# Half of the modulation vector moves from VectorE to TensorE, in the opening of a trunk kernel

## The chip, the cores and the metric

One NeuronCore of a Trainium2 chip runs the whole program. The time is device microseconds of one execution. PE is TensorE, DVE is VectorE, ACT is ScalarE, POOL is GpSimd, SP is SyncE, which here only issues DMAs.

## The reference, cut to what matters

One layer of a hybrid trunk: 2048 tokens, 1024 features, 8 heads of an RWKV7 mixer and 8 heads of chunked band attention. Its normalised input is scaled and shifted by a modulation vector that is made from a conditioning vector `c`:

```python
c_act = jax.nn.silu(c)
mod = c_act @ w_ada[l] + b_ada[l]                    # (1024) @ (1024, 3072)
shift, scale, gate = jnp.split(mod, 3, axis=-1)
h = rms_norm(x, norm_g[l]) * (1.0 + scale[:, None, :]) + shift[:, None, :]
proj = h @ w_in[l]
...
x = x + gate[:, None, :] * (y @ w_out[l])
```

So no token's projection can start before the parts of `shift` and `scale` that belong to its features are there. `w_ada` for shift and scale is 8 MB in f32.

## The kernel before

Features lie on partitions, in KT = 8 blocks of P = 128 (index k); tokens are taken 512 at a time. Matmuls of the projection keep f32 accuracy by splitting both operands into a high and a low part (`hh`, `hl` for h; `whi`, `wlo` for the weights) and making three 512-wide matmuls, lines L130 to L132, helper `gemm_k`.

`phase_a` projects and attends; `phase_r`, the recurrence, follows. Phase A's *opening* is what the change touches. It loads the first 512 tokens of x (eight tiles `hx`), sums their squares (`ssx` on DVE, `ps_ss` by four one-column matmuls on PE), takes the power -0.5 on POOL (`r`), spreads it over partitions (`rbx` on ACT, `ps_rx` by four transposes on PE, `rsb` on ACT), and multiplies all eight x tiles by it on POOL (`hx`, L309). Then a loop over k makes, for each block of features, two columns of the modulation vector `modv`, and with them h and its share of four projections that add up in the four PSUM tiles `ps_first`:

- `mod_part` loads two tiles `wada` of 128 x 1024 (half a megabyte each; seven buffers), scale first, then shift. In each, partition p holds the 1024 weights of output feature p, and DVE multiplies it by `sil`, which is silu(c) on every partition, and adds along the row (L146, a custom operation and a short read of the sum). L148 adds the bias.
- `g1` = (1 + scale) times the norm's gain (L405, DVE).
- `build_k` makes `hh` (ACT, L370), takes it from the full product (DVE, L371), and makes `hl` (ACT, L373).
- `split` loads the weights of this k (`raw`), and makes `whi` on ACT (L122) and `wlo` on POOL (L111).
- 12 wide matmuls: four projections, three products each.

The wada loads are issued from SP's queue, held behind the last load of x. Four casts of a zero tile into `pth` and `ptl` (L422, L423) stand behind the opening in the code, but belong to no step of it. Within phase A a scheduler sets the order of instructions on each engine when the kernel is built, by its own estimate of the times; on the chip each engine takes its instructions strictly in that order. Behind the opening PE goes on with the projections and the attention of the same tokens.

The gate half of `mod` is made much later, in `gate()`: DVE accumulates weights whose *input* features lie on partitions, times a column of `silc` (silu(c) with features on partitions), and PE adds over the partitions in one-column matmuls, `ps_gate`.

Of the kernel before, what the change touches and what calls it, by code (L numbers as in the profile page):

```python
# [9 lines left out]
F32 = mybir.dt.float32  # L10
F32R = mybir.dt.float32r
BF16 = mybir.dt.bfloat16
AF = mybir.ActivationFunctionType
ALU = mybir.AluOpType
# [4 lines left out]
P = 128  # L19
# [3 lines left out]
S = 2048  # L23
D = 1024
KT = D // P
# [47 lines left out]
def body(tc, nc, x, xT, wi, wadaT, wadaG, wo, sc, cst, bx, w2, a2, cb, eyes, outT):  # L73
    ctx = ExitStack()
    with ctx:
        pool = lambda name, st=ctx, **k: st.enter_context(tc.tile_pool(name=name, **k))
        cp = pool("cp", bufs=1)
        dp = pool("dp", bufs=1, space=DRAM)
        wx = pool("wx", bufs=2)
        psp = pool("psp", bufs=2, space=PSUM)  # L80

        y_d = dp.tile([NP, P, S], F32, name="y_d")
        ar_d = dp.tile([NP, P, 2 * S], F32, name="ar_d")
        kb_d = dp.tile([NP, P, 2 * S], F32, name="kb_d")
        bv_d = dp.tile([NP, P, S], F32, name="bv_d")
        v_d = dp.tile([NP, P, S], F32, name="v_d")
        sg_d = dp.tile([NP, P, S], F32, name="sg_d")

        sct = cp.tile([P, NSC], F32, name="sct")
        nc.sync.dma_start(out=sct, in_=sc)  # L90
        cs = cp.tile([P, NCP], F32, name="cs")
        nc.sync.dma_start(out=cs, in_=cst[:, 0:NCP])
        col = lambda n, i: sct[:, SC[n][0] + i:SC[n][0] + i + 1]
        cols = lambda n: sct[:, SC[n][0]:SC[n][1]]
        C = lambda n: cs[:, CS[n][0]:CS[n][1]]
        ident = C("ident")
        dv = cp.tile([P, 52], F32, name="dv")
        _d = [0]

        def derived(w):  # L100
            o = _d[0]
            _d[0] += w
            return dv[:, o:o + w]

        nhalf = cp.tile([P, 16], F32, name="nhalf")
        nc.gpsimd.memset(nhalf, -0.5)
        one = cp.tile([P, 1], F32, name="one")
        nc.gpsimd.memset(one, 1.0)

        def sub(eng, out, full, hi):  # L110
            eng.tensor_tensor(out=out, in0=full, in1=hi.bitcast(F32), op=ALU.subtract)  # L111

        ld1 = [None]

        def split_half(src, q):
            return split(src[:, q * 512:(q + 1) * 512])

        def split(src):
            raw = wx.tile([P, 512], F32, name="raw", tag="raw", bufs=3)
            ld1[0] = nc.sync.dma_start(out=(raw if len(src.shape) == 2 else raw.rearrange("p (a b) -> p a b", b=src.shape[2])), in_=src)  # L120
            hi = wx.tile([P, 512], F32R, name="whi", tag="whi", bufs=3)
            nc.scalar.copy(out=hi, in_=raw)  # L122
            lo = wx.tile([P, 512], F32R, name="wlo", tag="wlo", bufs=3)
            sub(nc.gpsimd, lo, raw, hi)
            return hi, lo

        def gemm_k(ps, w, h, k, kw, first, last):
            (wh, wl), (hh, hl) = w, h
            f = slice(kw * P, kw * P + P)
            nc.tensor.matmul(ps, lhsT=wh[:, f], rhs=hh[:, k, :], start=first, stop=False)  # L130
            nc.tensor.matmul(ps, lhsT=wh[:, f], rhs=hl[:, k, :], start=False, stop=False)  # L131
            nc.tensor.matmul(ps, lhsT=wl[:, f], rhs=hh[:, k, :], start=False, stop=last)  # L132

        def gemm(ps, src, h):
            ws = [split_half(src, q) for q in range(2)]
            for k in range(KT):
                gemm_k(ps, ws[k // 4], h, k, k % 4, k == 0, k == KT - 1)

        modv = cp.tile([P, 24], F32, name="modv")
        wcall = cp.tile([P, NP, S // 64], F32, name="wcall")  # L140

        def mod_part(wp, sil, ms):
            for m in ms:
                w = wp.tile([P, D], F32, name="wada", bufs=7)
                nc.sync.dma_start(out=w, in_=wadaT[m])
                nc.vector.tensor_tensor_reduce(out=w, in0=w, in1=sil, scale=1.0, scalar=0.0, op0=ALU.mult, op1=ALU.add,  # L146
                                               accum_out=modv[:, m:m + 1])
                nc.vector.tensor_tensor(out=modv[:, m:m + 1], in0=modv[:, m:m + 1], in1=col("bada", m), op=ALU.add)  # L148

        g1 = derived(8)  # L150
        q = phase_a(tc, nc, locals())
        phase_r(tc, nc, locals(), q)

# [131 lines left out]
def phase_a(tc, nc, e):  # L285
    x, xT, wi, bx, cst, cb, wadaG, w2, a2 = (e[k] for k in ("x", "xT", "wi", "bx", "cst", "cb", "wadaG", "w2", "a2"))
    C, col, cols, ident, derived = (e[k] for k in ("C", "col", "cols", "ident", "derived"))
# [4 lines left out]
    with st:  # L292
# [9 lines left out]
        def pst(name):  # L302
            return ps_t.tile([P, 512], F32, name=name, tag="pt")
# [28 lines left out]
        def load_x0():  # L332
            acc = W("ssx")
            xts = []
            for k in range(KT):
                t = W("hx")
                ld = nc.sync.dma_start(out=t, in_=xT[k, :, 0:TA])
                xts.append(t)
                sq = acc if k == 0 else ap.tile([P, 512], F32, name="sqx", tag="xt", bufs=2)
                nc.scalar.activation(sq, t, AF.Square)  # L340
                if k:
                    nc.vector.tensor_tensor(out=acc, in0=acc, in1=sq, op=ALU.add)
            ps = pst("ps_ss")
            for i in range(4):
                nc.tensor.matmul(ps[:, i:i + 1], lhsT=acc[:, i * P:(i + 1) * P], rhs=one, start=True, stop=True)
            s4 = ap.tile([P, 4], F32, name="s4", bufs=2)
            return xts, rms(s4, ps[:, 0:4]), ld
# [43 lines left out]
        mp = pool("mp", mst, bufs=1, side="right")  # L391
        sil = mp.tile([P, D], F32, name="sil")
        nc.sync.dma_start(out=sil, in_=cb)
        xts, rb0, ld0 = load_x0()
        sth = mp.tile([P, D], F32, name="sth", tag="wada", bufs=7)
        nc.scalar.activation(sth, sil, AF.Tanh, scale=0.5)
# [2 lines left out]
        rsb = finish_x(rb0)  # L399
        h0 = h_tiles()  # L400
        first = [psp.tile([P, 512], F32, name=f"ps_first{i}", tag="pj") for i in range(2)] + [pst("ps_first2"), pst("ps_first3")]
        with tc.issue_after(ld0.ins):
            for k in range(KT):
                mod_part(mp, sil, (8 + k, k))
                nc.vector.scalar_tensor_tensor(out=g1[:, k:k + 1], in0=modv[:, 8 + k:9 + k], scalar=1.0, in1=col("ng", k),  # L405
                                               op0=ALU.add, op1=ALU.mult)
                build_k(0, k, rsb, h0, xts[k])
                w = split(wi[17:30:4, :, k * P:(k + 1) * P].rearrange("f p c -> p f c"))
                for j in range(4):
                    gemm_k(first[j], w, h0, k, j, k == 0, k == KT - 1)  # L410
# [311 lines left out]
            nc.sync.dma_start(out=sg_d[p, :, tsl], in_=gr)  # L722

        def gate():
            silc = derived(8)
            nc.scalar.activation(silc, cols("c"), AF.Tanh, scale=0.5)
            nc.vector.tensor_scalar(out=silc, in0=silc, scalar1=0.5, scalar2=0.5, op0=ALU.mult, op1=ALU.add)
            nc.vector.tensor_tensor(out=silc, in0=silc, in1=cols("c"), op=ALU.mult)
            for hf in range(2):
                acc = W("gacc")  # L730
                for k in range(KT):
                    w = wx.tile([P, 512], F32, name="raw", tag="raw", bufs=3)
                    nc.sync.dma_start(out=w, in_=wadaG[k, :, hf * 512:hf * 512 + 512])
                    if k == 0:
                        nc.vector.tensor_scalar(out=acc, in0=w, scalar1=silc[:, 0:1], scalar2=None, op0=ALU.mult)
                    else:
                        nc.vector.scalar_tensor_tensor(out=acc, in0=w, scalar=silc[:, k:k + 1], in1=acc, op0=ALU.mult, op1=ALU.add)
                    if k % 2 == 1:
                        yield
                ps = pst("ps_gate")  # L740
                for m in range(4):
                    nc.tensor.matmul(ps[:, m:m + 1], lhsT=acc[:, m * P:(m + 1) * P], rhs=one, start=True, stop=True)
                o = 16 + 4 * hf
                nc.vector.tensor_tensor(out=modv[:, o:o + 4], in0=ps[:, 0:4], in1=cols("bada")[:, o:o + 4], op=ALU.add)
                yield
# [371 lines left out]
def layout(a):  # L1117
# [12 lines left out]
    dist = 128 + np.arange(P)[:, None] - np.arange(256)[None, :]  # L1130
    idx = np.clip(dist, -63, 128) + 63
    return {
        "x": x.reshape(16, P, D), "xT": x.T.reshape(KT, P, S), "wi": wt(f["w_in"][0]), "wadaT": f["w_ada"][0].T.reshape(24, P, D)[:16], "wadaG": f["w_ada"][0][:, 2 * D:].reshape(KT, P, D),
        "wo": wt(f["w_out"][0]), "sc": np.concatenate([parts[n] for n in SC], axis=1), "cst": consts(),
        "cb": np.broadcast_to(f["c"][0], (P, D)), "bx": rb[:, idx].transpose(1, 0, 2), "w2": f["w2"][0], "a2": f["a2"][0],
        "eyes": np.repeat(np.eye(32, dtype=np.float32).reshape(16, 2, 32).transpose(1, 0, 2).reshape(2, 512), 64, axis=0),
# [19 lines left out]
```

## Time and profile before

| | |
|---|---|
| median of 3 executions | 1775.95 us (1772.7 to 1777.89) |
| the profiled execution | 1771.38 us, span 1769.6 us |
| last matmul of the opening ends | 64.53 us |
| PE busy in the span | 1553.7 us, 88% |
| DVE busy in the span | 1090.2 us, 62% |

The profile is that of one execution. The span is from its first to its last recorded instruction; starts are counted from its beginning. A row of the timeline gives the start, the busy time, engine, line, operation, the tiles written and read, shapes, how many instructions it sums up, and in brackets how long the engine stood idle before it and what released it. An f32 matmul leaves two records, an fp32r one leaves one. Matmuls overlap in the pipeline: what one costs in a dense run is the distance between starts.

### The profile page before, as it was taken

The page shows a single profiled execution, that of the slowest core. Times are in us where ns is not written, and L with a number is a line of the kernel's source. Part 1 is how long each engine was busy: PE and PEld are TensorE (multiplying, and loading weights), DVE is VectorE, ACT ScalarE, POOL GpSimd, SP SyncE. Part 2 cuts the span into 40 slices and gives each one's busy share as a digit, 9 for nine tenths or more (in the row PEclk, how much of TensorE's full clock was granted, in tenths as well). Part 3 has the DMA queues.
Part 4 walks back from the last instruction along what each step waited for, and adds up shares of the span by engine and source line. Part 5 has one row for each costly group of instructions (what it writes and reads, how often), then busy time and mean ns, then how long its engine had stood idle before and what let it go on. Part 6 is the DMA issues. An engine that isn't in the chain of part 4 may idle for free. (4 is left out here: it accounts for less than half of the span.)

```text
span 1769.6 us, 32130 instructions
## 1 busy us (share of the span) xinstructions
PE 1553.7 (88%) x11944; PEld 1270.9 (72%) x11944; DVE 1090.2 (62%) x2407; ACT 929.9 (53%) x2087; POOL 708.4 (40%) x571
## 2 busy tenths in 40 slices
PE   3899998899999899999979999978688889889795
PEld 2677876678777678888868878856576667767685
DVE  7647457475576846746566574576555576566732
ACT  3666556566555565656566666652234344444440
POOL 4455544555444455444536544505212121221221
PEclk9999999899999999999999999999788999899897
DMA  8463333332324523223142332255746665664532
GB/s 286 130 222 102 100 114 101 114 119 73 113 93 135 167 72 125 81 93 114 60 137 72 126 102 66 66 192 159 229 129 183 167 195 154 187 183 122 148 115 90
DMA packets 188957, 231.60 MB, mean 131 GB/s; under 512 B 62976, under 2 KB 101632, under 8 KB 188800
## 3 DMA queue, kind: packets, MB, share of 16 engines
q1 hardware_dynamic: 183552, 212.76, 39.6%
q0 software_dynamic: 5248, 16.78, 2.7%
q8 instruction: 94, 1.54, 0.4%
q14 instruction: 63, 0.52, 0.1%
HBM read 171.30 MB, written 58.20 MB: 130 GB/s over the span
## 5 line engine op out<-in xcount | busy, mean ns | idle before, releaser
L111 POOL TENSOR_TENSOR wlo<-raw,whi 128x512 fp32r<-128x512 f32 x272 | 369.9, 1364 | 424.4 <-ACT whi L122 374.9
L122 ACT CAST whi<-raw 128x512 fp32r<-128x512 f32 x272 | 167.6, 618 | 173.9 <-issue 53.5
L130 PE MATMUL ps_r<-hh,whi 128*128 128x512 f32 x544 | 219.5, 404 | 13.8 <-ACT carry L632 10.6
L132 PE MATMUL ps_r<-hh,wlo 128*128 128x512 f32 x544 | 218.1, 401 | 2.2 <-POOL wlo L111 2.2
L131 PE MATMUL ps_r<-hl,whi 128*128 128x512 f32 x544 | 218.1, 401 | 0.0
L130 PE MATMUL ps_qkvg<-hh,whi 128*128 128x512 f32 x480 | 196.0, 410 | 10.7 <-ACT carry L632 7.1
L131 PE MATMUL ps_qkvg<-hl,whi 128*128 128x512 f32 x480 | 194.4, 406 | 9.0 <-DVE hl L377 5.3
L132 PE MATMUL ps_qkvg<-hh,wlo 128*128 128x512 f32 x480 | 192.7, 402 | 0.4 <-POOL wlo L111 0.4
L111 DVE TENSOR_TENSOR ptl<-ps_pt,pth 128x384 fp32r<-128x384 f32 (+1 forms) x232 | 105.2, 473 | 43.5 <-ACT pth L598 42.9
L130 PEld LDWEIGHTS ps_r<-hh,whi 128*128 128x128 f32 x544 | 103.5, 190 | 34.8 <-ACT carry L632 11.4
L588 ACT ACTIVATE sp<-sp,mn 128x640 f32<-128x640 f32 (+4 forms) x128 | 97.9, 765 | 53.9 <-DVE mn L584 53.0
L132 PEld LDWEIGHTS ps_r<-hh,wlo 128*128 128x128 f32 x544 | 103.3, 190 | 24.8 <-POOL wlo L111 3.1
L131 PEld LDWEIGHTS ps_r<-hl,whi 128*128 128x128 f32 x544 | 103.5, 190 | 20.1
L130 PEld LDWEIGHTS ps_qkvg<-hh,whi 128*128 128x128 f32 x480 | 92.0, 192 | 32.8 <-ACT carry L632 8.5
L131 PEld LDWEIGHTS ps_qkvg<-hl,whi 128*128 128x128 f32 x480 | 91.9, 191 | 31.1 <-DVE hl L377 7.5
L598 ACT CAST pth<-ps_pt 128x384 fp32r<-128x384 f32 (+1 forms) x232 | 90.8, 416 | 42.8 <-PE ps_pt L595 39.9
L132 PEld LDWEIGHTS ps_qkvg<-hh,wlo 128*128 128x128 f32 x480 | 92.2, 192 | 21.0 <-POOL wlo L111 0.6
L595 PE MATMUL ps_pt<-cs,sp 128*128 128x128 f32 x560 | 94.5, 281 | 10.8 <-DVE ptl L111 4.3
L604 PE MATMUL ps_o<-ptl,vc 128*128 128x256 f32 x336 | 92.5, 301 | 9.5 <-DVE ptl L111 9.5
L603 PE MATMUL ps_o<-pth,vc 128*128 128x256 f32 x336 | 92.2, 295 | 8.2 <-ACT pth L598 5.9
L1019 POOL DMA_DIRECT2D out<-xres x40 | 22.3, 557 | 173.3 <-DVE xres L1018 131.6
L582 DVE CUSTOM_DVE_ANT_0 sp<-ps_sa,mab 128x384 f32<-128x384 f32 (+1 forms) x112 | 58.7, 524 | 43.4 <-PE ps_sa L558 26.8
(256 smaller groups left out, 3713.5 us busy)
## 6 DMA issues: line engine op xcount, KB each, us to landing
raw<-in_wi SPq DMA_DIRECT2D x264, 256.0 KB, 2.9
hx<-in_xT SPq DMA_DIRECT2D x32, 256.0 KB, 5.4
wada<-in_wadaT SPq DMA_DIRECT2D x16, 512.0 KB, 8.7
ar_d<-art SPq DMA_DIRECT2D x16, 512.0 KB, 3.7
kb_d<-kbt SPq DMA_DIRECT2D x16, 512.0 KB, 3.2
kb<-kb_d SPq DMA_DIRECT2D x8, 1024.0 KB, 5.9
ar<-ar_d SPq DMA_DIRECT2D x8, 1024.0 KB, 6.4
xres<-in_xT SPq DMA_DIRECT2D x32, 256.0 KB, 3.4
```

Of the source, the lines that this page charges most:

```text
L111: eng.tensor_tensor(out=out, in0=full, in1=hi.bitcast(F32), op=ALU.subtract)
L122: nc.scalar.copy(out=hi, in_=raw)
L130: nc.tensor.matmul(ps, lhsT=wh[:, f], rhs=hh[:, k, :], start=first, stop=False)
L131: nc.tensor.matmul(ps, lhsT=wh[:, f], rhs=hl[:, k, :], start=False, stop=False)
L132: nc.tensor.matmul(ps, lhsT=wl[:, f], rhs=hh[:, k, :], start=False, stop=last)
L582: nc.vector.tensor_tensor_reduce(out=sp[:, 0:na], in0=sa[:, 0:na], in1=m_ap, scale=1.0, scalar=3e38, op0=ALU.add, op1=ALU.min, accum_out=m ...
L588: nc.scalar.activation(sp[:, 0:n], sp[:, 0:n], AF.Exp, scale=-1.0, bias=mn[:, 1:2], accum_out=ls[:, 2 * v + hh_:2 * v + hh_ + 1])
L595: nc.tensor.transpose(pp[:, kk - lo, :], sp[:, kk * P:(kk + 1) * P], ident)
L598: nc.scalar.copy(out=ph, in_=pp)
L603: nc.tensor.matmul(po[:, hh_, :], lhsT=wv_, rhs=pth[:, m, :], start=(m == m0), stop=False)
L604: nc.tensor.matmul(po[:, hh_, :], lhsT=wv_, rhs=ptl[:, m, :], start=False, stop=(m == 5))
L1019: nc.gpsimd.dma_start(out=dst[m, :, tsl], in_=xt)
```

## The change

The host lays out the scale half of `w_ada` with the input features on partitions. `mod_part` then makes the scale column of block k on PE: eight f32 matmuls, each with a 128 x 128 piece of the weight tile as stationary operand and one column of `silc` as moving operand, add up in column k of one PSUM tile, `ps_mod`. The bias add reads that column (L152). The shift half is made as before. `silc` is made ahead of the opening rather than in `gate()`.

```diff
-        def mod_part(wp, sil, ms):
-            for m in ms:
-                w = wp.tile([P, D], F32, name="wada", bufs=7)
-                nc.sync.dma_start(out=w, in_=wadaT[m])
-                nc.vector.tensor_tensor_reduce(out=w, in0=w, in1=sil, scale=1.0, scalar=0.0, op0=ALU.mult, op1=ALU.add,
-                                               accum_out=modv[:, m:m + 1])
-                nc.vector.tensor_tensor(out=modv[:, m:m + 1], in0=modv[:, m:m + 1], in1=col("bada", m), op=ALU.add)
+        def mod_part(wp, sil, silc, ps, k):
+            w = wp.tile([P, D], F32, name="wada", bufs=7)
+            nc.sync.dma_start(out=w, in_=wadaT[8 + k])
+            for i in range(KT):
+                nc.tensor.matmul(ps[:, k:k + 1], lhsT=w[:, i * P:(i + 1) * P], rhs=silc[:, i:i + 1], start=(i == 0), stop=(i == KT - 1))
+            w = wp.tile([P, D], F32, name="wada", bufs=7)
+            nc.sync.dma_start(out=w, in_=wadaT[k])
+            nc.vector.tensor_tensor_reduce(out=w, in0=w, in1=sil, scale=1.0, scalar=0.0, op0=ALU.mult, op1=ALU.add,
+                                           accum_out=modv[:, k:k + 1])
+            nc.vector.tensor_tensor(out=modv[:, k:k + 1], in0=modv[:, k:k + 1], in1=col("bada", k), op=ALU.add)
+            nc.vector.tensor_tensor(out=modv[:, 8 + k:9 + k], in0=ps[:, k:k + 1], in1=col("bada", 8 + k), op=ALU.add)
...
+        silc = derived(8)
+        nc.scalar.activation(silc, cols("c"), AF.Tanh, scale=0.5)
+        nc.vector.tensor_scalar(out=silc, in0=silc, scalar1=0.5, scalar2=0.5, op0=ALU.mult, op1=ALU.add)
+        nc.vector.tensor_tensor(out=silc, in0=silc, in1=cols("c"), op=ALU.mult)
...
+        ps_mod = pst("ps_mod")
         with tc.issue_after(ld0.ins):
             for k in range(KT):
-                mod_part(mp, sil, (8 + k, k))
+                mod_part(mp, sil, silc, ps_mod, k)
...
         def gate():
-            silc = derived(8)
-            nc.scalar.activation(silc, cols("c"), AF.Tanh, scale=0.5)
-            nc.vector.tensor_scalar(out=silc, in0=silc, scalar1=0.5, scalar2=0.5, op0=ALU.mult, op1=ALU.add)
-            nc.vector.tensor_tensor(out=silc, in0=silc, in1=cols("c"), op=ALU.mult)
```

The scheduler sets a new order. On PE, at the start of the program, this stood before; the names are the PSUM tile written, then the moving and the stationary operand, and the brackets name the engines and DMA queues waited for:

```order
L345 MATMUL ps_ss<-one,ssx 128x1 x3
L319 MATMUL ps_rx<-cs,rbx 128x128 [waits DMAHW1_49,Activation_49]
L319 MATMUL ps_rx<-cs,rbx 128x128 x3
L130 MATMUL ps_first_163<-hh,whi 128x512 [waits Activation_49]
L130 MATMUL ps_first_164<-hh,whi 128x512
```

This stands there now:

```order
L323 MATMUL ps_rx<-cs,rbx 128x128 [waits DMAHW1_49,Activation_49]
L323 MATMUL ps_rx<-cs,rbx 128x128 x3
L146 MATMUL ps_mod<-dv,wada 128x1 [waits DMAHW3_49]
L146 MATMUL ps_mod<-dv,wada 128x1 x7
L146 MATMUL ps_mod<-dv,wada 128x1 [waits DMAHW6_49,DVE_49]
L146 MATMUL ps_mod<-dv,wada 128x1 x7
L130 MATMUL ps_first_166<-hh,whi 128x512 [waits Activation_49]
L130 MATMUL ps_first_167<-hh,whi 128x512
```

Two columns of `ps_mod` come ahead of the first wide matmul, and the second column, like each later one, begins with a wait for DVE. On DVE, in the middle of the opening, this stood before:

```order
L146 ISA wada,modv<-wada,sil 128x1024 [waits DMAHW1_49]
L146 ISA modv 128x1
L422 CAST pth<-zero 128x128 [waits Pool_49]
L423 CAST pth<-zero 128x128
L422 CAST ptl<-zero 128x128
L423 CAST ptl<-zero 128x128
L148 TENSOR_TENSOR modv<-modv,sct 128x1 [waits DVE_49]
L146 ISA wada,modv<-wada,sil 128x1024 [waits DMAHW2_49]
L146 ISA modv 128x1
L405 SCALAR_TENSOR_TENSOR dv<-modv,sct 128x1 [waits DVE_49]
L371 SCALAR_TENSOR_TENSOR hx<-hx,dv,hh 128x512 [waits Activation_49]
```

This stands there now; `sct` holds the biases and `dv` is where `g1` lies:

```order
L149 ISA wada,modv<-wada,sil 128x1024 [waits DMAHW7_49]
L149 ISA modv 128x1
L431 CAST pth<-zero 128x128 [waits Pool_49]
L432 CAST pth<-zero 128x128
L431 CAST ptl<-zero 128x128
L432 CAST ptl<-zero 128x128
L151 TENSOR_TENSOR modv<-modv,sct 128x1 [waits DVE_49]
L149 ISA wada,modv<-wada,sil 128x1024 [waits DMAHW2_49]
L149 ISA modv 128x1
L152 TENSOR_TENSOR modv<-ps_mod,sct 128x1 [waits PE_49]
L151 TENSOR_TENSOR modv<-modv,sct 128x1 [waits DVE_49]
L414 SCALAR_TENSOR_TENSOR dv<-modv,sct 128x1 [waits DVE_49]
```

The casts now follow the second reduction where they followed the fifth, and L152 of column 0 stands behind them and behind the third reduction.

## Rows read from the trace of the kernel before

**Rows 1.** The page's totals: busy time, share of the span, instructions.

```profile
PE 1553.7 (88%) x11944; PEld 1270.9 (72%) x11944; DVE 1090.2 (62%) x2407; ACT 929.9 (53%) x2087; POOL 708.4 (40%) x571
```

**Rows 2.** Windows, us: length, busy PE, PEld, DVE, ACT, POOL; granted clock, DMA share, GB/s.

```profile
21.70:35.30 13.60, 3.19 (x9) 1.88 (x9) 12.19 (x12) 3.83 (x6) 13.05 (x10) 1.00 0.92 327
35.30:64.50 29.20, 25.09 (x94) 19.23 (x94) 25.61 (x46) 16.36 (x27) 12.87 (x9) 0.94 0.51 149
64.50:75.00 10.50, 10.50 (x75) 8.53 (x75) 1.71 (x5) 5.84 (x12) 8.28 (x6) 1.00 0.34 100
75.00:85.00 10.00, 5.32 (x24) 4.22 (x23) 6.92 (x11) 7.62 (x15) 5.10 (x4) 0.88 0.43 134
105.00:115.00 10.00, 6.82 (x22) 4.99 (x21) 7.76 (x14) 5.58 (x16) 4.52 (x4) 0.83 0.92 299
```

**Rows 3.** Windows of DVE's operations on tile wada: DVE busy, clock, DMA share, GB/s.

```profile
0.00:64.50 64.50, 20.93 (x16) 0.97 0.73 241
15.10:24.30 9.20, 6.59 (x5) 1.00 1.06 382
```

**Rows 4.** Timeline of DVE in the opening.

```profile
16.33 0.16 DVE L148 TENSOR_TENSOR modv<-modv,sct 128x1 f32<-128x1 f32 x1
...
18.36 1.74 DVE L146 CUSTOM_DVE_ANT_0 wada<-wada,sil 128x1024 f32<-128x1024 f32 x1 [0.52 <-DMA wada<-in_wadaT]
...
24.34 1.27 DVE L422 CAST pth<-zero 128x128 fp32r<-128x128 f32 x1 [1.29 <-POOL zero L418]
...
31.53 1.21 DVE L405 SCALAR_TENSOR_TENSOR dv<-modv,sct 128x1 f32<-128x1 f32 x1
32.66 1.83 DVE L371 SCALAR_TENSOR_TENSOR hx<-hx,dv,hh 128x512 f32<-128x512 f32 x1
```

**Rows 5.** Timeline of POOL in the opening.

```profile
18.98 2.02 POOL L352 TENSOR_TENSOR r<-s,nhalf 128x4 f32<-128x4 f32 x1
...
24.27 11.34 POOL L309 TENSOR_TENSOR hx<-hx,rsb 128x512 f32<-128x512 f32 x8
```

**Rows 6.** Timeline of PE: one-column f32 matmuls and the transposes of the opening.

```profile
15.29 1.84 PE L345 MATMUL ps_ss<-one,ssx 128*128 128x1 f32 x8 [15.29 <-DVE ssx L342]
21.71 1.12 PE L319 MATMUL ps_rx<-cs,rbx 128*128 128x128 f32 x4 [4.57 <-ACT rbx L354]
...
564.30 0.95 PE L742 MATMUL ps_gate<-one,gacc 128*128 128x1 f32 x8
```

**Rows 7.** Timeline of PE: wide matmuls of the opening.

```profile
38.58 1.09 PE L130 MATMUL ps_first<-hh,whi 128*128 128x512 f32 x4
...
54.32 0.50 PE L130 MATMUL ps_first<-hh,whi 128*128 128x512 f32 x1 [3.18 <-ACT whi L122]
...
57.11 1.82 PE L132 MATMUL ps_first<-hh,wlo 128*128 128x512 f32 x4
58.77 1.09 PE L130 MATMUL ps_first<-hh,whi 128*128 128x512 f32 x4
59.70 1.09 PE L131 MATMUL ps_first<-hl,whi 128*128 128x512 f32 x4
...
64.13 0.40 PE L132 MATMUL ps_first<-hh,wlo 128*128 128x512 f32 x1
```

**Rows 8.** Timeline of ACT and DVE: steps of the chains.

```profile
21.04 0.62 ACT L354 COPY rbx<-r 128x512 f32<-128x512 f32 x1 [3.36 <-POOL r L352]
...
58.92 0.82 ACT L370 ACTIVATE hh<-hx,modv,dv 128x512 fp32r<-128x512 f32 x1 [0.51 <-DVE dv L405]
...
59.84 0.75 DVE L371 SCALAR_TENSOR_TENSOR hx<-hx,dv,hh 128x512 f32<-128x512 f32 x1 [0.82 <-ACT hh L370]
...
60.67 0.72 ACT L373 ACTIVATE hl<-hx,modv 128x512 fp32r<-128x512 f32 x1
```

**Rows 9.** Timeline behind the opening: POOL, and DVE reading PSUM beside it.

```profile
69.86 2.92 POOL L503 TENSOR_TENSOR rq<-ms,nhalf 128x16 f32<-128x16 f32 x1
70.15 0.42 DVE L111 TENSOR_TENSOR vc<-ps_vt,vc 128x256 fp32r<-128x256 f32 x1 [0.82 <-ACT vc L522]
```

More of the change, by code (lines that the diff above doesn't have):

```diff
@@ L1132, in layout @@
     return {
-        "x": x.reshape(16, P, D), "xT": x.T.reshape(KT, P, S), "wi": wt(f["w_in"][0]), "wadaT": f["w_ada"][0].T.reshape(24, P, D)[:16], "wadaG": f["w_ada"][0][:, 2 * D:].reshape(KT, P, D),
+        "x": x.reshape(16, P, D), "xT": x.T.reshape(KT, P, S), "wi": wt(f["w_in"][0]), "wadaT": np.concatenate([f["w_ada"][0][:, :D].T.reshape(KT, P, D), f["w_ada"][0][:, D:2 * D].reshape(KT, P, KT, P).transpose(2, 1, 0, 3).reshape(KT, P, D)]), "wadaG": f["w_ada"][0][:, 2 * D:].reshape(KT, P, D),
         "wo": wt(f["w_out"][0]), "sc": np.concatenate([parts[n] for n in SC], axis=1), "cst": consts(),
```

## The prediction

> **What bounds the kernel now.** I read the page's engine totals first: PE is busy 88% of the span, DVE 62% [rows 1]. So time put onto PE counts wherever PE has no idle time to take it in, and time taken off DVE counts only where DVE is what PE waits for. The edit lies in the opening of phase A, so the windows of that stretch come next [rows 2]. Before 21.70 us PE does almost nothing. From 21.70 to 35.30 it is busy 3.19 us while DVE and POOL are nearly full. From 35.30 to 64.50 DVE is busy 25.61 of 29.20 us and PE 25.09, at a granted clock of 0.94. From 64.50 to 75 PE is busy for all of 10.50 us, and only then do stretches with PE idle time return. In the opening, then, DVE comes first and PE close behind it, and whoever moves work from one to the other must see what it costs on each. The windows of the tile wada say what DVE would shed: 16 reductions take 20.93 us, 1.31 us each [rows 3].
>
> The lines of DVE and POOL show why DVE is so full. While POOL multiplies eight tiles in one block of 11.34 us [rows 5], DVE's tiniest operations take 1.2 us, such as L405 at 31.53, against 0.16 us for L148 at 16.33; the four casts between 24.34 and 31.53 take 1.3 us each, and the 512-wide L371 takes 1.83 us where it takes 0.75 elsewhere [rows 4, 8]. DVE and POOL take turns there, one operation each. The last matmul of the opening ends at 64.13 + 0.40 = 64.53 us [rows 7].
>
> **The change part by part.** *Removed:* eight reductions on DVE, 8 x 1.31 = 10.5 us. The bias add of the scale half stays, with PSUM as its first input. The trace does not show it, so I bound it: 0.16 us as L148 takes alone, 1.21 us as L405 takes in POOL's block [rows 4]. I take 0.16, because the vc operation, which reads PSUM too, takes 0.42 us for 256 columns while POOL runs a tensor operation [rows 9]. The Trainium skill ("SBUF — State Buffer", section "Who interferes with whom") says that a DVE operation with two SBUF inputs contends with a GpSimd (POOL) operation that reads SBUF and one with at most one such input does not. By that rule 0.16 holds, and the trace agrees on both halves; were the new add hit as well, the one that falls in POOL's block would cost 1.1 us more.
>
> *Added on PE:* 64 f32 matmuls of one column. The nearest rows are ps_ss and ps_gate, of the same form, two records to a matmul. Four of ps_ss take 1.84 us at 15.29, 0.46 each, after PE stood idle; four of ps_gate take 0.95 us in the middle of dense work, 0.24 each [rows 6]. Wide matmuls show the same two levels: from 57.11 to 58.77 four start 0.42 us apart, from 58.77 to 59.70 four start 0.233 us apart [rows 7], the factor near two between 1.2 and 2.4 GHz. So 64 of them cost 15 us at the high level and 29 us at the low one.
>
> *Added as a wait:* all eight columns go into one PSUM tile, ps_mod. By the order of instructions, the first matmul of each later column waits for DVE, that is for L152 of the column before, and L152 waits for PE. PE and DVE now go hand in hand, and every wide matmul of PE stands behind it in PE's queue.
>
> *Moved:* silc's three small operations go from the gate to the opening (DVE's two no larger than L148's 0.16 us, and before the x tiles are in, while PE has nothing to do; worth nothing). On POOL the pow of rms comes ahead of the first wlo, where it now ends at 18.98 + 2.02 = 21.00 beside DVE's custom reduction [rows 4, 5].
>
> **The chain, step by step.** ps_ss ends at 17.13 us as before [rows 6]. DVE 0.16, POOL's pow alone about 1 us (an estimate: half of its 2.02 beside DVE), ACT's rbx 0.62 [rows 8], ps_rx 1.12 [rows 6] with about 0.1 between: ps_rx ends near 20.1, where it ended at 22.83. The first column follows at the low level, 8 x 0.46 = 3.7: 23.8 us. Now DVE. Its second reduction needs the fourth wada tile; the third landed at 18.36 [rows 4], and 0.5 MB at 382 GB/s [rows 3] is 1.35 us, so it runs 19.7 to 21.0. Behind it stand the four casts, a bias add and the third reduction, as they stood from 24.34 to 31.6, 7.3 us [rows 4], and again in POOL's block, which follows ps_rx. So L152 of column 0 comes at about 28.4 and PE waits from 23.8 to 28.4. Column 1 takes to 32.1. By then L414 and L371 (two DVE operations, 1.2 and 1.83) with ACT's hh and hl (0.82, 0.72) [rows 4, 8] have given hl at about 34.2; the other eight wide matmuls at 0.42 end the first feature block at 37.6.
>
> What remains is 48 narrow and 84 wide matmuls: at the high level 48 x 0.25 + 84 x 0.233 = 12.0 + 19.6 = 31.6 us, which ends at 69.2 with no wait at all. Before, the same 84 wide ones ran from 38.58 to 64.53 [rows 7], that is 25.9 us, 6.3 us of it waits and low clock. DVE is lighter now, which shortens these; the new handshake lengthens them: from L152 on, a feature block needs L414, hh, L371 and hl, of which the last three ran from 58.92 to 61.39 [rows 8], before its last matmuls can go. I take 8.5 us for waits and low-level stretches together, between 0 and twice that. The opening then ends near **77.7 us, 13 us later** than now; 69.2 (+4.7) without waits.
>
> Bounds: were even the first block at the high level, 56 narrow and 96 wide matmuls from 28.4 on end at 28.4 + 14.0 + 22.4 = 64.8 (no gain). With all that remains at the low level, 48 x 0.46 + 84 x 0.42 = 57.4 us ends at 95.0 (+30.5).
>
> **What comes back.** Directly behind, PE is full [rows 2], so nothing. From 75 to 85 and from 105 to 115 PE is idle 4.7 and 3.2 us [rows 2], where it waits for other engines that are now no later than they were, or for DMAs. Work that comes late to PE closes such gaps. I take half of these 7.9 us, 4 us, with 0 and all of it as bounds. Sum: 13 - 4 = **+9 us**. The profiled execution took 1771.38 us, span 1769.6, 4.6 us under the median of 1775.95; against the median the forecast is 1785 us. A measurement here can tell about 0.3%, 5.3 us, from no change.
>
> **Rivals.** *Faster, PE takes it for nothing.* From 21.70 to 64.50 PE is idle 42.80 - 28.28 = 14.5 us [rows 2], as much as 64 narrow matmuls cost at the high level, and DVE, the busier one, sheds 10.5. If DVE sets the pace throughout, the opening ends some 10 us earlier: 1766. For it the DVE share speaks; against it that most of PE's idle time lies before 38 us, while the handshake holds six of the eight columns until after that. It needs narrow matmuls under about 0.15 us each (28.4 + 56 x 0.15 + 22.4 = 59.2) or a second column that starts near 22 us. Chance 0.10.
>
> *Given back.* The opening is 5 to 13 us late but the gaps up to 115 us take 7.9 us or more, or the high level holds throughout: +1, about 1777. PE's idle time further on (12% of the span) speaks for it, its full stretch behind the opening against it. Chance 0.29.
>
> *PE stays at the low level.* Narrow matmuls between short groups of wide ones might keep PE low, as the matmuls from 57.11 to 58.77 were, a few us after PE had stood idle for 3.18 us [rows 7]. Then +30.5 - 4 = +26.5: 1802. Against it, ps_gate was at the high level amid dense work [rows 6], and wide groups are still two thirds of PE's time here. Chance 0.08. The Trainium skill ("TensorE: Matmul & The Clock Gate", section "HAM oscillation — how this bites in real kernels") describes short bursts of matmuls that each start at the low clock because of the waits between them; here it would be this rival, and the trace bears it out for one stretch only.
>
> **How the numbers follow.** The likeliest, chance 0.53, is slower by 5.3 to 20 us around +9: 1785. The range 1774 to 1798 leaves out most of the faster rival and of the low-clock one. Faster 0.10; same 0.29; slower 0.53 + 0.08 = 0.61.
>
> **What would show it.** In the profile after: a wait of PE for DVE's L152 of some 4 us before 29 us, shorter ones ahead of later columns; L152 at 0.16 us; narrow matmuls at 0.46 early and about 0.25 later; DVE's share of the opening down by about 10 us; the last ps_first near 78 us; PE full after it. Wrong it would be if the casts run ahead of POOL's block, so that column 1 starts by 25, if the narrow ones cost under 0.15 us, or if a reordered stretch further on moves the end by itself.

## The result, and the profile after

The changed kernel took 1788.0 us (median of 6 runs) against 1776.24 us for the kernel before (6 runs); the ratio is 1.0056, 95% interval 1.0034 to 1.0078, that is some 10 us more (6 to 14). One of the six executions, at 1849 us with a mean granted clock of 0.816, is left out of the ratio. The profiled execution took 1787.82 us, 16.4 us more than that of before, which was itself 4.9 us under its median.

The page's totals of the changed kernel, for [rows 1]: PE gained 35 us of busy time and DVE lost 20.

```profile
PE 1588.5 (89%) x12072; PEld 1306.7 (73%) x12072; DVE 1069.9 (60%) x2391; ACT 930.6 (52%) x2087; POOL 705.4 (39%) x571
```

The timeline of PE in the opening:

```profile
19.32 1.12 PE L323 MATMUL ps_rx<-cs,rbx 128*128 128x128 f32 x4 [2.09 <-ACT rbx L358]
20.22 3.41 PE L146 MATMUL ps_mod<-dv,wada 128*128 128x1 f32 x16
25.00 3.57 PE L146 MATMUL ps_mod<-dv,wada 128*128 128x1 f32 x16 [1.36 <-DVE modv L152]
28.43 2.05 PE L130 MATMUL ps_first<-hh,whi 128*128 128x512 f32 x4
...
32.37 0.39 PE L132 MATMUL ps_first<-hh,wlo 128*128 128x512 f32 x1
...
40.97 3.11 PE L146 MATMUL ps_mod<-dv,wada 128*128 128x1 f32 x16 [2.21 <-DVE modv L152]
...
59.59 1.62 PE L146 MATMUL ps_mod<-dv,wada 128*128 128x1 f32 x14
61.46 3.12 PE L146 MATMUL ps_mod<-dv,wada 128*128 128x1 f32 x16 [0.25 <-DVE modv L152]
64.44 2.05 PE L130 MATMUL ps_first<-hh,whi 128*128 128x512 f32 x4
...
76.10 2.08 PE L130 MATMUL ps_first<-hh,whi 128*128 128x512 f32 x4 [2.16 <-ACT hh L374]
...
80.10 0.39 PE L132 MATMUL ps_first<-hh,wlo 128*128 128x512 f32 x1
```

The opening ends at 80.10 + 0.39 = 80.49 us, 16.0 later than before [rows 7]. A column of ps_mod is 16 records. Two columns stand ahead of the first wide matmul, as the order said, and the second waits for L152, but for 1.36 us only. At 59.59 seven matmuls take 1.62 us, 0.23 each, while from 61.46 eight take 3.12. The waits of PE from 17 to 80.5 us (the engine, the tile, what released it; total us, times, longest):

```profile
PE ps_mod L146 <- DVE modv L152: 3.8, 3, 2.2
PE ps_first L130 <- ACT hh L374: 2.2, 1, 2.2
PE ps_rx L323 <- ACT rbx L358: 2.1, 1, 2.1
PE ps_first L132 <- POOL wlo L111: 1.3, 1, 1.3
```

Windows of all engines, for those of [rows 2]:

```profile
35.30:64.50 29.20, 25.74 (x114) 22.71 (x114) 12.54 (x25) 10.41 (x16) 10.81 (x8) 0.72 0.58 158
```

DVE is busy 12.54 us where it was 25.61, so the relief came. PE is as busy as before, at a granted clock of 0.72 where it was 0.94. Windows of PE alone (length, PE busy, granted clock, DMA share, GB/s) say where the clock fell, and what came behind the opening:

```profile
32.80:80.50 47.70, 41.82 (x182) 0.75 0.40 112
...
41.00:49.00 8.00, 8.00 (x36) 0.53 1.01 282
49.00:55.20 6.20, 6.20 (x16) 0.50 0.45 106
55.20:61.40 6.20, 6.01 (x35) 1.00 0.24 69
61.40:68.80 7.40, 7.34 (x26) 0.54 0.16 48
```

```profile
80.50:91.00 10.50, 10.50 (x74) 1.00 0.16 50
91.00:101.00 10.00, 5.32 (x25) 0.93 0.44 134
```

About half speed, the 1.2 GHz level, was granted for two long stretches, 41 to 55 us and 61.4 to 68.8; a short one, where four matmuls take 2.08 us at 76.10, follows a wait of 2.16 us. The first long one follows a wait of 2.21 us. Ahead of the second PE was hardly idle: it is busy for 6.01 of the 6.20 us before it. What it did just before the clock fell is the run of narrow matmuls from 59.59 on. The last two rows are, 16 us later, the same picture as before [rows 2]: 10.5 us full, then a stretch with 5.32 us busy in 10.

From 32.8 to 80.5 the 47.7 us of PE are 15.3 us of busy time in narrow matmuls (95 records), 5.9 of waits, and 26.5 left for the 84 wide ones, which take 19.6 at the high level.

### The profile page after: what moved, and what is told of

Same layout as the page of the kernel before. It is cut to its first block, busy times and chain, and to the rows that moved or that the text cites. A ratio compares the mean times of both kernels' runs of the same rounds, so it can differ in the third digit from the quotient of the medians.

```text
span 1786.1 us, 32383 instructions
## 1 busy us (share of the span) xinstructions
PE 1588.5 (89%) x12072; PEld 1306.7 (73%) x12072; DVE 1069.9 (60%) x2391; ACT 930.6 (52%) x2087; POOL 705.4 (39%) x571
## 5 line engine op out<-in xcount | busy, mean ns | idle before, releaser
L111 POOL TENSOR_TENSOR wlo<-raw,whi 128x512 fp32r<-128x512 f32 x272 | 366.2, 1350 | 414.4 <-ACT whi L122 372.7
L122 ACT CAST whi<-raw 128x512 fp32r<-128x512 f32 x272 | 167.8, 618 | 194.9 <-issue 61.4
L604 PEld LDWEIGHTS ps_pt<-cs,sp 128*128 128x128 f32 x560 | 68.7, 144 | 25.4 <-ACT sp L597 5.4
```

What stands on the lines that cost most here:

```text
L604: nc.tensor.transpose(pp[:, kk - lo, :], sp[:, kk * P:(kk + 1) * P], ident)
```

## The experiments

All are compared with the kernel before, run on the same chip. "Opening" is the end of the last ps_first matmul in the one profile of each.

| kernel | opening ends, us | ratio to before, 95% interval |
|---|---|---|
| before | 64.53 | |
| changed | 80.49 | 1.0056 (1.0034 to 1.0078) |
| 1 one of eight matmuls | 58.74 | 0.9994 (0.9968 to 1.0019) |
| 2 four PSUM tiles | 77.78 | 1.0066 (1.0040 to 1.0091) |
| 3 64 columns | 73.43 | 1.0030 (0.9999 to 1.0061) |
| 4 silc alone | 64.29 | 1.0015 (0.9986 to 1.0045) |
| 5 two columns on PE | 65.46 | 1.0001 (0.9972 to 1.0030) |
| 6 row form | 70.44 | 1.0030 (1.0004 to 1.0056) |
| 7 four tiles, 64 columns | 72.32 | 1.0045 (1.0027 to 1.0062) |
| 8 before, casts on ACT | 62.54 | 0.9991 (0.9969 to 1.0013) |
| 9 five columns on PE | 71.65 | 1.0035 (1.0010 to 1.0061) |
| 10 two columns, 64 wide, casts on ACT | 64.75 | 1.0032 (1.0009 to 1.0056) |
| 11 one column, 64 wide, casts on ACT | 63.67 | 0.9960 (0.9937 to 0.9984) |
| 12 the same again | 62.90 | 0.9958 (0.9935 to 0.9981) |

**1. One matmul of eight.**

```diff
-            for i in range(KT):
-                nc.tensor.matmul(ps[:, k:k + 1], lhsT=w[:, i * P:(i + 1) * P], rhs=silc[:, i:i + 1], start=(i == 0), stop=(i == KT - 1))
+            nc.tensor.matmul(ps[:, k:k + 1], lhsT=w[:, 0:P], rhs=silc[:, 0:1], start=True, stop=True)
```

> Each scale column is made of one matmul instead of eight (the scale comes from the first 128 inputs only); loads, PSUM tile, L152 and the wait of each column for the one before stay. Theory A, PE's time: the 64 narrow matmuls hold PE for 22.3 us, 15.3 of it behind the first feature block, and the wide ones beside them run partly at the low clock (about 7 us). Seven eighths of it go: the opening, which ends at 80.5 us in the changed kernel and at 64.5 in the one before, ends between 59 and 66, and the program takes 0.995 to 1.002 of the time before. Theory B, the handshake between PE and DVE through one PSUM tile: the waits stay, the opening ends above 72 and the ratio stays at 1.004 or more.

The opening ends at 58.74, just past the lower edge of theory A, with PE's waits for L152 grown to 6.5 us in total. So the waits as such don't cost it: PE's matmuls do. Against the kernel before it shows what the relief of DVE is worth at this place when PE gets little to do, 5.8 us. Yet the ratio is 0.9994. Its PE timeline behind the opening:

```profile
57.65 1.09 PE L132 MATMUL ps_first<-hh,wlo 128*128 128x512 f32 x4
60.72 1.02 PE L472 MATMUL ps_sm<-cs,sq 128*64 128x2 f32 x16 [1.98 <-ACT sq L500]
...
62.69 0.63 PE L132 MATMUL ps_r<-hh,wlo 128*128 128x512 f32 x1
63.12 0.63 PE L130 MATMUL ps_r<-hh,whi 128*128 128x512 f32 x1
...
76.78 1.04 PE L322 MATMUL ps_rb<-cs,rb 128*128 128x128 f32 x8
```

and the window in it, PE alone:

```profile
61.60:67.40 5.80, 5.80 (x18) 0.50 0.44 136
```

PE waits 1.98 us for ACT's sq, which stands in ACT's queue behind work on nb and three whi, and then runs 5.8 us at half clock, matmuls 0.43 us apart. ps_rb, which began at 77.5 us in the kernel before, begins at 76.78: of 5.8 us 0.7 are left.

**2. Four PSUM tiles.**

```diff
-        ps_mod = pst("ps_mod")
+        ps_mods = [pst("ps_mod")] + [p.tile([P, 512], F32, name=f"ps_mod{t}", tag=t) for p, t in ((ps_s, "sa"), (ps_s, "sb"), (ps_o, "o"))]
...
-                mod_part(mp, sil, silc, ps_mod, k)
+                mod_part(mp, sil, silc, ps_mods[k % 4], k)
```

> The columns go in turn into four PSUM tiles, so that a column waits only for the one four before it; all 64 matmuls stay. Theory A, PE's time: only PE's waits for L152 (3.8 us in the changed kernel) and some of what follows from them can go: the opening ends between 74 and 78, ratio 1.003 to 1.008. Theory B, the handshake: the opening ends near 65 and the ratio is within 0.3% of 1.

Waits of PE from 17 to 78 us:

```profile
PE ps_first L130 <- ACT hh L374: 2.4, 2, 1.9
PE ps_modsa L146 <- DMA wada<-in_wadaT: 0.9, 1, 0.9
PE ps_first L132 <- POOL wlo L111: 0.6, 1, 0.6
PE ps_first L131 <- ACT hl L377: 0.4, 1, 0.4
```

No wait for L152 is left, and the opening ends 2.7 us earlier, which the ratio doesn't show. The 2.7 us are not the price of the handshake alone, since PE's order changed with it: the fifth to seventh columns and the start of the eighth now follow each other.

```profile
48.69 1.61 PE L146 MATMUL ps_mod<-dv,wada 128*128 128x1 f32 x14
50.17 2.98 PE L146 MATMUL ps_modsa<-dv,wada 128*128 128x1 f32 x16
53.01 3.55 PE L146 MATMUL ps_modsb<-dv,wada 128*128 128x1 f32 x16
```

This stretch of PE's timeline shows the clock fall with no idle time just ahead of it. PE is busy without a gap from 46.26 to 57.4 us. Seven one-column matmuls take 1.61 us (0.23 each), the eight of the next column 2.98, and the eight behind them 3.55 (0.44 each). From 50.5 to 64.5 us the granted clock is 0.51.

**3. 64 columns.**

```diff
-                nc.tensor.matmul(ps[:, k:k + 1], lhsT=w[:, i * P:(i + 1) * P], rhs=silc[:, i:i + 1], start=(i == 0), stop=(i == KT - 1))
+                nc.tensor.matmul(ps[:, 64 * k:64 * k + 64], lhsT=w[:, i * P:(i + 1) * P], rhs=silc[:, i, :], start=(i == 0), stop=(i == KT - 1))
...
-            nc.vector.tensor_tensor(out=modv[:, 8 + k:9 + k], in0=ps[:, k:k + 1], in1=col("bada", 8 + k), op=ALU.add)
+            nc.vector.tensor_tensor(out=modv[:, 8 + k:9 + k], in0=ps[:, 64 * k:64 * k + 1], in1=col("bada", 8 + k), op=ALU.add)
...
+        silw = mp.tile([P, KT, 64], F32, name="silw")
+        nc.scalar.copy(out=silw, in_=silc.unsqueeze(2).broadcast_to([P, KT, 64]))
...
-                mod_part(mp, sil, silc, ps_mod, k)
+                mod_part(mp, sil, silw, ps_mod, k)
```

> The same 64 matmuls in number and weights, but each streams silc's column 64 times over, into 64 columns of PSUM of which one is read. Theory C, the clock falls because one-column matmuls keep PE busy without streaming columns: the wide matmuls at 0.43 us (about 33 of 96 in the changed kernel) become few after the first block, and narrow ones take about 0.24 throughout, so the opening ends at 70 to 74 in spite of the added columns. Without it (the clock falls for PE's waits, which stay): the low stretches stay and the opening ends at 80 or later.

The PE timeline at the place where the changed kernel fell to half clock:

```profile
60.90 2.00 PE L146 MATMUL ps_mod<-silw,wada 128*128 128x64 f32 x16 [0.25 <-DVE modv L152]
62.99 1.20 PE L130 MATMUL ps_first<-hh,whi 128*128 128x512 f32 x4
64.02 1.89 PE L146 MATMUL ps_mod<-silw,wada 128*128 128x64 f32 x16
...
66.04 0.39 PE L132 MATMUL ps_first<-hh,wlo 128*128 128x512 f32 x1
66.27 0.40 PE L131 MATMUL ps_first<-hl,whi 128*128 128x512 f32 x1
```

and the window behind the first feature block, PE alone:

```profile
33.70:73.50 39.80, 35.95 (x186) 0.87 0.44 133
```

The same 64 matmuls over the same weights, each with more to do, and the opening ends 7.1 us earlier. After 60 us a column takes 2.0 us (3.12 in the changed kernel), behind the same wait of 0.25 us, and wide matmuls stay 0.23 apart. The mean granted clock behind the first block is 0.87 (0.75). One low stretch is left behind the first block, from 44 to 53 us, after a wait of PE of 3.5 us, so the low stretches became fewer, not few. Of the 8 us less behind the first block, 4.9 are in the wide matmuls, 1.0 in the narrow ones and 2.1 in waits.

**4. silc alone.** Its three operations stand ahead of the opening, as in the change, in the kernel before.

> The kernel before with silc's three operations moved to the opening, and nothing else. Theory A: the opening ends at 64.5 within 1 us and the time is that of before within 0.3%. Rival, the time comes from the order that the scheduler sets anew and not from the matmuls: a shift of 5 us or more.

64.29 and 1.0015: no change that can be told, as expected. The move of silc and the new order that goes with it explain nothing of the 16 us. Its profiled execution is also a warning: it ended some 10 us behind that of the kernel before, nearly all of it gathered after 560 us, with a ratio that cannot be told from 1. Positions in two single traces are compared below only up to 333 us.

**5. Two columns on PE, six on DVE.** `mod_part` takes the old path where k is 2 or more; the host lays out the weights accordingly.

```diff
+                if m >= 8 and k < 2:
+                    for i in range(KT):
+                        nc.tensor.matmul(ps[:, k:k + 1], lhsT=w[:, i * P:(i + 1) * P], rhs=silc[:, i:i + 1], start=(i == 0), stop=(i == KT - 1))
+                    nc.vector.tensor_tensor(out=modv[:, m:m + 1], in0=ps[:, k:k + 1], in1=col("bada", m), op=ALU.add)
+                else:
...
```

> Only the first two scale columns are made on PE, where PE is idle anyway (before its first wide matmul); the other six stay on DVE as before. Theory A: PE's added work costs only where PE has no idle time, so the opening ends no later than before, at 60 to 65 us, and the program takes the time before within 0.3%: an opening that ended 5.8 us early in the first experiment was only 0.7 us early 13 us later. Rival, any column on PE costs its 2.5 us: the opening ends at 69.

```profile
28.36 3.57 PE L148 MATMUL ps_mod<-dv,wada 128*128 128x1 f32 x16 [4.76 <-DVE modv L149]
31.80 2.05 PE L130 MATMUL ps_first<-hh,whi 128*128 128x512 f32 x4
```

As theory A has it, within half a microsecond of its edge: both columns lie ahead of the first wide matmul (the rows are PE's timeline of the second) and the ratio is 1.0001. Here the second column does wait 4.76 us for DVE, since a bias add, one more reduction and g1, 1.1 to 1.2 us each, stand ahead of the add that it waits for.

**6. Row form.** silc is the stationary operand and the weights stream; all eight scale tiles load first.

```diff
+            for i in range(KT):
+                w = mp.tile([P, D], F32, name="wada", bufs=7)
+                nc.sync.dma_start(out=w, in_=wadaT[8 + i])
+                for q in range(2):
+                    nc.tensor.matmul(ps_row[q][0:1, :], lhsT=silc[:, i:i + 1], rhs=w[:, q * 512:(q + 1) * 512], start=(i == 0), stop=(i == KT - 1))
...
+            for k in range(KT):
+                nc.tensor.matmul(ps_mod[:, k:k + 1], lhsT=mrow[:, k * P:(k + 1) * P], rhs=one[0:1, :], start=True, stop=True)
...
```

> The scale half is made on PE for all features at once, with silc's columns as stationary operand and the weights streaming: 16 f32 matmuls of 512 columns into one row of PSUM, two copies by ACT, eight one-column matmuls that turn the row into columns, one bias add and one g1 for all blocks; the eight scale tiles load ahead of the shift tiles. Theory A with C (narrow matmuls cost PE 22 us and leave it at the low clock): PE's added work is 7 to 14 us, before the wide matmuls begin, and DVE keeps its relief; the opening ends between 50 and 62. Program: 0.994 to 0.998 if an earlier opening is passed on, 0.998 to 1.001 if it is lost behind it as in the first experiment. Rival, the loss came from putting PE ahead of DVE in the chain at all: the opening ends above 66.

```profile
25.49 0.66 PE L318 MATMUL ps_rx<-cs,rbx 128*128 128x128 f32 x4
...
31.32 1.94 PE L417 MATMUL ps_mod<-one,mrow 1*128 1x1 f32 x16
43.50 2.07 PE L130 MATMUL ps_first<-hh,whi 128*128 128x512 f32 x4 [10.24 <-ACT hh L369]
```

```profile
28.52 2.02 DVE L145 CUSTOM_DVE_ANT_0 wada<-wada,sil 128x1024 f32<-128x1024 f32 x1 [9.72 <-DMA wada<-in_wadaT]
```

A miss: 70.44, on the rival's side, and a ratio of 1.0030. The 16 streaming matmuls did cost 0.86 us each and are done by 31.3. But the scheduler put ps_rx (PE's timeline, first fence) between them, 6 us later than in the changed kernel, and POOL's block of eight products starts behind it, at 28.20. The shift tiles load behind the eight scale tiles, so DVE's first reduction there starts at 28.52 (its timeline, second fence), and its small operations fall into POOL's block. The bias add stands behind four reductions and runs at 42.18; PE waits 10.24 us. So the length of PE's new work is not what ended the opening late. Which of the two did, the late ps_rx or the late shift tiles, no run parts.

**7. Four tiles and 64 columns together.**

> Four PSUM tiles in turn and 64 columns to each narrow matmul, both together. If handshake (2.7 us) and clock (7.1 us) add, the opening ends at 69 to 72 and the ratio is 1.000 to 1.004. What is then left over the kernel before is the number of the narrow matmuls alone: some 64 at 0.24 us less what PE's idle time takes in. If either alone had hidden the other, it ends at 73 to 78.

72.32, 0.3 us past the upper edge for a sum of both, with a ratio of 1.0045 that lies past its edge too; beside experiment 3 the four tiles bring 1.1 us, alone they brought 2.7. The fifth to seventh columns stand back to back as in experiment 2. There the clock fell; here, with 64 columns to a matmul, it does not: the eight that took 3.55 us take 1.95.

```profile
49.22 1.95 PE L146 MATMUL ps_modsb<-silw,wada 128*128 128x64 f32 x16
```

No wait for L152 is left, and 8 us over the kernel before are. They are not the number of narrow matmuls alone, as was expected: PE waits 3.79 us for ACT's hh, and from 55.6 to about 64 us, behind that wait, it runs at half clock.

**8. The kernel before with the casts of the zero tile on ACT.**

```diff
-            nc.vector.tensor_copy(out=t[:, 0, P:256], in_=zero)
-            nc.vector.tensor_copy(out=t[:, 5, 0:P], in_=zero)
+            nc.scalar.copy(out=t[:, 0, P:256], in_=zero)
+            nc.scalar.copy(out=t[:, 5, 0:P], in_=zero)
```

> The kernel before with the four casts of the zero tile on ACT in place of DVE, where they took 5.2 us in POOL's block. Theory A says DVE bounds the opening of the kernel before until 38 us: the opening ends 2 to 5 us earlier, at 60 to 63. The program: within 0.3%, as in the first experiment. If DVE's relief is worth nothing there, it ends at 64.5.

62.54 and 0.9991: the opening gains 2.0 us of the 5.2 that DVE sheds, and the time of the program cannot be told from that of before.

**9. Five columns on PE**, as experiment 5 with 5 for 2.

> Five of the eight scale columns on PE, three on DVE: the dose between the second column (opening ends at 65.5 us) and the eighth (80.5). Theory A with C: three more columns than in the fifth experiment cost 8 to 9 us of narrow and slowed wide matmuls where PE has little idle time; the opening ends at 70 to 76, and the ratio is 1.001 to 1.005. If the loss were one event (a single late wait), it ends at either 65 or 80.

71.65. With none, two, five and eight columns on PE the opening ends at 64.5, 65.5, 71.7 and 80.5: nearly nothing for the first two, then 2 to 3 us a column. It is a dose, not one event.

**10, 11 and 12. What was cheap, together.** Columns on PE only for k below 2 (10) or 1 (11 and 12), with 64 columns streamed, and the casts on ACT.

> The first two scale columns on PE with 64 columns streamed, six on DVE, and the four casts on ACT: what was cheap in each experiment. The opening ends at 58 to 63. Program: 0.997 to 1.000, a gain of some 2 us that the interval may not part from none, since an opening that ends early has so far come back within 4 us of the kernel before.

> The same with one column on PE, so that no column waits for another before the first wide matmul (4.8 us in the fifth experiment). The opening ends at 57 to 62, program 0.997 to 1.000.

> The kernel of the eleventh experiment once more, since its ratio of 0.996 has no counterpart in its profile, where the opening ends 0.9 us before that of the kernel before and the positions up to 1130 us differ by 2.5 us at most. If the gain is the kernel's, the ratio is again under 0.998 with an interval clear of 1. If it came from the draw of runs, the ratio is 0.998 to 1.002.

With one column the kernel is faster than before by 0.4%, twice, a little more than expected, though the openings of 11 and 12 end later than the 62 us that were expected at most. With two it is slower by 0.3%, against the expectation, and its opening, at 64.75, misses it too. The profiles don't show why: the openings of 11 and 12 end 0.9 and 1.6 us earlier than that of before, and at 333 us they are 2.1 and 2.6 us ahead; that of 10 ends 0.2 us later and is 0.2 us ahead there. Where the other 5 us of the gain lie, and the 6 us of the loss, stays open; the profiled executions of 11 and 12 took 1776.1 and 1776.8 us, more than the medians of their runs (1769 and 1763 us), and may not contain it.

## Why the prediction was right

The sign and the mechanism held: PE's added work and the low clock cost more than DVE's relief gives. The size (+9 forecast, +10 measured, interval 6 to 14) is luck in part. The first feature block was put 4.8 us too late, waits and low clock 7.6 us too small, and what is given back some 2 us too small; the three nearly cancel.

**Right.** ps_rx ended at 20.44 (20.1 forecast) and the first column at 23.6 (23.8). The narrow matmuls cost 0.43 us early and 0.23 in dense work (0.46 and 0.24 to 0.25). DVE's busy time up to the end of the opening went from 51.24 to 38.38 us (about 10 less forecast). L152 takes 0.15 us in POOL's block, at 24.79, where L151, of the same size, takes 1.24 (timelines of DVE and of POOL):

```profile
20.87 0.22 DVE L431 CAST pth<-zero 128x128 fp32r<-128x128 f32 x1
...
21.14 0.22 DVE L431 CAST ptl<-zero 128x128 fp32r<-128x128 f32 x1
21.28 1.29 DVE L432 CAST ptl<-zero 128x128 fp32r<-128x128 f32 x1
22.49 1.24 DVE L151 TENSOR_TENSOR modv<-modv,sct 128x1 f32<-128x1 f32 x1
23.65 1.21 DVE L149 CUSTOM_DVE_ANT_0 wada<-wada,sil 128x1024 f32<-128x1024 f32 x1
...
24.79 0.15 DVE L152 TENSOR_TENSOR modv<-ps_mod,sct 128x1 f32<-128x1 f32 x1
```

```profile
21.13 12.91 POOL L313 TENSOR_TENSOR hx<-hx,rsb 128x512 f32<-128x512 f32 x8 [0.37 <-ACT rsb L364]
```

The rule on SBUF inputs by which the prediction chose that price holds for this add. It does not hold for every operation with one SBUF input, as the prediction words it: the casts have one, and took 1.27 us and more in POOL's block [rows 4].

**Too late by 4.8 us: the first feature block.** "Behind it stand the four casts ... and again in POOL's block" took the casts at 1.3 us each. The timeline of DVE above shows three of the four at 0.2: POOL's block began at 21.13, and the third started at 21.14. L152 came at 24.8, not 28.4, PE waited 1.36 us, not 4.6, and the first block ended at 32.8, not 37.6. The rest of the 4.8 us came after, inside the block: its last matmuls start 0.23 us apart, and the sum had 0.42. The prediction named casts ahead of POOL's block, and column 1 by 25 us, as a sign that it was wrong. Column 1 did start at 25.00, and the opening ended late all the same: the sign touched the first block alone, and the loss lies behind it.

**Too small by 7.6 us: "8.5 us for waits and low-level stretches together".** Measured, these are 47.7 - 31.6 = 16.1 us: 5.9 of waits, 6.9 by which the wide matmuls exceed the high level and 3.3 by which the narrow ones do, near the upper bound of 17 that stood beside the 8.5. In the sum the clock fell for idle time alone, as in [rows 7], and the rival had narrow matmuls keep it low. The changed kernel shows it falling around 62 us, with PE idle 0.25 us, during narrow matmuls; experiment 2 shows the same with no idle time. Experiments 3 and 7 show that the same matmuls with 64 columns leave it high at these places. So the low-clock rival, at 8%, had a part in the truth: a mean clock of 0.75 behind the first block is half of that time at the low level.

The Trainium skill ("TensorE: Matmul & The Clock Gate", section "HAM oscillation — how this bites in real kernels") puts such falls down to waits between bursts. That agrees with the low stretch from 44 to 53 us in experiment 3, behind 3.5 us of idle time; the one at 62 us in the changed kernel and the one at 51 us in experiment 2 came without such a wait. The prediction saw one such stretch in the trace of before; that trace has more, with matmuls 0.43 us apart from 35.89 us on, behind 6.79 us of idle time, and from 83.79 on, behind 4.68.

**Given back: not where it was put.** The forecast gave back 4 us of the opening by 115 us. By the ratio 6 of the 16 us are given back in the whole program (2 to 10 by its interval; the 16 are read from one profile of each). Two positions in the changed kernel's PE timeline; the same matmuls start at 77.48 and 332.63 us before:

```profile
93.43 0.60 PE L323 MATMUL ps_rb<-cs,rb 128*128 128x128 f32 x4
...
346.25 0.52 PE L473 MATMUL ps_sm<-cs,sq 128*64 128x2 f32 x12
```

So 15.9 us late, and then 13.6: 2.3 us came back up to here, and where the rest did is not shown. Up to 101 us nothing comes back: the stretch with 5.32 us busy [rows 2] has moved by 16 us and is as long as before. PE's wait in it is for ACT's carry, 4.68 us in both kernels, so it seems to follow from PE's own work. The kernels that were late by 5.9 to 15.9 us at ps_rb (experiments 2, 3, 6, 7, 9 and the changed kernel) are late by 9.2 to 13.6 at 333 us: the distances there don't go over one to one, in either direction. That half of two windows' idle time would return was a guess without a mechanism.

**The faster rival** was wrong. It had DVE's relief bring the opening some 10 us forward; where PE got little to do (experiment 1) it was worth 5.8 us, and 13 us later 0.7: there ACT's queue and the low clock behind it took most of the gain. That is not so of every early opening. Those of experiments 8 and 12, 2.0 and 1.6 us early, are still 1.7 and 1.6 us early at ps_rb. An opening that ends late is passed on to ps_rb in every kernel here, since PE is full up to there. So a large gain was worth less at this place than a loss of the same size, and no line of the prediction said so.

## What to carry to other kernels

Moving work to an engine with idle time pays by place: two columns lay in PE's idle time and cost 1 us, eight cost 16. Ask of a one-column matmul what it costs in PE's time (0.23 to 0.45 us here, for a 128 x 128 piece of the weights and one column), and what it does to the clock of the wide matmuls beside it. And before counting a gain, look at what the next stage needs beside it: of the 5.8 us won in experiment 1, 0.7 were left 13 us later.

## What the runs showed of the hardware that was not expected

- PE fell to half clock while it was busy: around 62 us of the changed kernel, during a run of one-column f32 matmuls, with 0.25 us of idle time, and around 51 us of experiment 2 with none. With 64 columns in each the clock stayed up at these places (experiments 3 and 7), and a column cost 2.0 us where it had cost 3.12, and 1.95 where it had cost 3.55.
- An f32 matmul with 64 moving columns costs about what one with a single column costs: 16 records in 1.89 to 2.00 us at the high level, 0.24 to 0.25 us per matmul, against 0.23.
- The granted clock in the windows reads 1.00 for 20 to 28.5 us of the changed kernel, while a column there takes 3.41 us, the price of the low level; the distance between starts tells it, the clock column does not, early in a program.
